# A two-layer decoder trunk on one core: the first layer's head, from the first load to the second chunk of the input projection

## The chip, the cores and the metric

The kernel runs on one core of a Trainium2 chip. Its time is in device microseconds (us), the median of several runs: 663.21 (662.91 to 663.65, three runs). The profile is one further execution, with a time of its own.

## The reference

Two layers over 256 tokens of 1024 channels, float32. Each layer normalises x (RMS norm with a gain), projects it once into 2866 columns, feeds three mixers in parallel from these columns, projects back, adds to x, and runs an MLP with squared ReLU:

```python
for l in range(DEPTH):                       # DEPTH = 2
    h = rms_norm(x, ln1_gain[l])
    proj = h @ w_in[l]                       # (256, 1024) @ (1024, 2866)
    ... = jnp.split(proj, offsets, axis=-1)  # q, six k/v, gates | c_q, c_kv, k_pe | retention q, k, v, gate
    o_nsa = nsa_mixer(partial_rope(nsa_q, cos_p, sin_p), ...)       # compressed, selected, window branches
    o_mla = mla_mixer(mla_cq, mla_ckv, mla_kpe, ..., cos_m, sin_m)  # low-rank queries and keys
    o_ret = retention_mixer(ret_q, ret_k, ret_v, ret_gate, ..., cos_r, sin_r)
    x = x + jnp.concatenate([o_nsa, o_mla, o_ret], axis=-1) @ w_out[l]
    h = rms_norm(x, ln2_gain[l])
    x = x + jnp.square(jax.nn.relu(h @ w_up[l])) @ w_down[l]
return rms_norm(x, final_gain)
```

The rotary tables cos and sin are computed from the positions, for three widths.

## The kernel before, in words

The 256 tokens are two tiles of 128 (t = 0, 1). x stays in SBUF (`xs`, 128 partitions x 2 x 1024). Matmuls in full float32 precision are made of three products (`mm3`, L145): each operand is split into a high part, cast to fp32r on ScalarE (L141), and a low part, the difference, on VectorE (L142); the sum of low x high, high x low and high x high goes into one PSUM bank.

The input projection goes by chunks of columns: A (434: gates, low-rank queries and keys), B2 (384), B1, B3, then the retention's. A chunk's weights come in units (`raw` tiles): A has four, each of two blocks of 128 rows (2 x 434 columns), B2 four of 2 x 384. For each unit and each token tile `inproj` (L549) does two `mm3`, so chunk A is 48 products. Behind A come the low-rank weights uq and uk (scaled by a norm gain and split, L389 and L390), B2, the small loads for the compression (`add_cmp`, L398: sixteen position loads of 8 KB and three of 32 KB), and so on.

`Stream` (L266) holds all units in order. `get` loads up to 12 units ahead of the one asked for, on SyncE's queue, and has those up to four ahead split. Raw tiles have five buffers, split tiles five, and a load waits for a buffer. `hold` and `release` keep splits behind a given instruction. The order of instructions on each engine is made when the program is built, from simulated times and from priorities (`prio`); `tc.issue_after` puts an instruction behind another.

The head, before: SyncE issues the constants `c0s` (with the identity for transposes), half of x's first tile, the gain `g8`, the other half, A's unit 0, x's whole second tile, A's units 1 to 3 (L168 to L180, L324). TensorE does eight warm-up matmuls on a zeroed tile `idle` (L177). `norm_half` (L481) transposes x by 512 channels of a tile: four transposes into a bank, a multiplication by the transposed gain `gT` on VectorE (`xg`, L494), and a split into `xT`. All four halves are done so, in the order (t, h) = (0,0), (0,1), (1,0), (1,1); the sums of squares follow on ScalarE (`sum_sq`, L504), the rows' factors on POOL, and then, in program order ahead of chunk A, the rotary tables (`rope_tables`, L201: some 28 short VectorE instructions and two Sins). Since the normalising factor is applied when a chunk is evacuated (`scaled`, L563), the products need only `xT`. The low parts of A's units 1 and 2 are on POOL (`START_POOL`, L49).

Of the kernel before, what the change touches and what calls it, by code (L numbers as in the profile page):

```python
# [48 lines left out]
START_POOL = (1, 2)  # L49
# [28 lines left out]
def tile_hybrid_trunk(  # L78
# [66 lines left out]
    def mm3(o, a, b, start, stop):  # L145

        nc.tensor.matmul(o, a[1], b[0], start=start, stop=False)  # L147
        nc.tensor.matmul(o, a[0], b[1], start=False, stop=False)  # L148
        nc.tensor.matmul(o, a[0], b[0], start=False, stop=stop)  # L149
# [16 lines left out]

    g8 = scr("g8", [8, P])
    nc.sync.dma_start(c0s, c0)  # L168
    nc.sync.dma_start(xs[:, 0, 0:512], xv[:, 0, 0:512])
    nc.sync.dma_start(g8, ln1_gain[0].rearrange("(k p) -> k p", p=P))  # L170
    nc.sync.dma_start(xs[:, 0, 512:D], xv[:, 0, 512:D])

    idle = scr("idle", [P, P])
    nc.vector.memset(idle, 0.0)
    ps_idle = acc("ps_idle")
    for _ in range(WARM):
        nc.tensor.matmul(ps_idle[:, 0:P], idle, idle, start=True, stop=True)  # L177

    def late_start():
        nc.sync.dma_start(xs[:, 1, :], xv[:, 1, :])  # L180

    nc.gpsimd.dma_start(pos_i, positions.rearrange("o (t p) -> p (o t)", p=P))
# [18 lines left out]
    def rope_tables():  # L201
# [27 lines left out]
        nc.scalar.activation(s1, r, AF.Sin)  # L229
        nc.scalar.activation(s2, r, AF.Sin, scale=0.5)  # L230
        nc.vector.tensor_tensor(u, s2, s2, op=ALU.mult)
        nc.vector.tensor_scalar(u, u, -2.0, 1.0, op0=ALU.mult, op1=ALU.add)
        for off, sl, n in ((0, slice(0, 16, 2), 8), (16, slice(0, 16), 16), (48, slice(16, 48), 32)):
            for half in range(2):
                dst = slice(off + half * n, off + (half + 1) * n)
                nc.vector.tensor_copy(tab_c[:, :, dst], u[:, :, sl])
                nc.vector.tensor_scalar(tab_s[:, :, dst], s1[:, :, sl], 1.0 if half else -1.0, None, op0=ALU.mult)
# [28 lines left out]
    class Stream:  # L266
# [21 lines left out]

        def hold(self, key):

            self.limit = self.index[key]
# [25 lines left out]
    def add_unit(key, pieces, n, eng=nc.vector):  # L317

        name = "_".join(str(z) for z in key)

        def load():
            raw = raw_tile(name)
            for view, src in pieces:
                nc.sync.dma_start(view(raw), src)  # L324
            return raw

        def split_(raw):
            p = hilo(name)
            m = n // PIECES.get('A0' if key[:2] == (0, 'A') else key[1], 1)
            for o in range(0, n, m):  # L330
                split(p[0][:, o:o + m], p[1][:, o:o + m], raw[:, o:o + m], eng)
            return p

        W.add(key, load, split_)
# [12 lines left out]
    def add_chunk(l, name, end=None, first=0):  # L347
        col, n = CHUNKS[name]
        wv = w_in[l].rearrange("(k p) n -> p k n", p=P)
        for i, ks in list(enumerate(KSETS[n]))[first:end]:  # L350
            m = len(ks)
            add_unit((l, name, i), [(lambda r_, m=m, n=n: r_[:, 0:m * n].rearrange("p (k n) -> p k n", k=m),
                                     wv[:, ks[0]:ks[-1] + 1, col:col + n])], m * n,
                     nc.gpsimd if (l, name) == (0, "A") and i in START_POOL else nc.vector)
# [6 lines left out]
    def add_mla(l):  # L361
        def small():
            nrm = p2.tile([P, 4], F32, name=f"l{l}_nrm", tag="nrm")
            nc.sync.dma_start(nrm[:, 0:2], mla_q_norm[l].rearrange("(k p) -> p k", p=P))
            nc.sync.dma_start(nrm[:, 2:3], mla_kv_norm[l].rearrange("(k p) -> p k", p=P))
            return nrm

        add_side(l, "nrm", small)

        def load_uq():  # L370
            raw = raw_tile(f"uq{l}")
            nc.sync.dma_start(raw[:, 0:960].rearrange("p (k n) -> p k n", k=2),
                              mla_w_uq[l].rearrange("(k p) n -> p k n", p=P))
            return raw

        def load_uk():
            raw = raw_tile(f"uk{l}")
# [20 lines left out]
    def add_cmp(l):  # L398
        def small():
            w2s = p1.tile([P, 3, 64], F32, name=f"l{l}_w2s", tag="w2s")  # L400
            pos_t = p1.tile([P, 2, 2, 64], F32, name=f"l{l}_pos_t", tag="pos_t")
            for z, (pe, w2) in enumerate(((cmp_pos_k, cmp_w2_k), (cmp_pos_v, cmp_w2_v))):
                nc.sync.dma_start(w2s[:, 2 * z], w2[l])
                for rep in range(8):
                    nc.sync.dma_start(pos_t[rep * 16:(rep + 1) * 16, z], pe[l].rearrange("(b a) d -> a b d", b=2))
            nc.sync.dma_start(w2s[:, 1], cmp_w2_k[l])
# [40 lines left out]
    for l in range(DEPTH):  # L447
        if l == 0:
            add_chunk(l, "A", 1)
            W.add("x1", late_start)  # L450
            add_chunk(l, "A", 4, 1)
        else:
            add_chunk(l, "A")
        add_mla(l)
        add_chunk(l, "B2")
# [25 lines left out]
    def norm_half(t, h, gain, eng=nc.vector):  # L481
# [3 lines left out]
        if gain is None:  # L485
            for j in range(4):
                nc.tensor.transpose(ps[:, j * P:(j + 1) * P], xs[:, t, h * 512 + j * P:h * 512 + (j + 1) * P], ident)
            if t == h == 0:

                ps_g = acc("ps_g")  # L490
                nc.tensor.transpose(ps_g[:, 0:8], g8, ident[0:8, 0:8])
                nc.vector.tensor_copy(gT, ps_g[:, 0:8])
            xg = xg.rearrange("p (k c) -> p k c", k=4)
            nc.vector.tensor_tensor(xg, ps.rearrange("p (k c) -> p k c", k=4),  # L494
                                    gT[:, 4 * h:4 * h + 4].unsqueeze(2).broadcast_to([P, 4, P]), op=ALU.mult)
            dst = (slice(None), slice(4 * h, 4 * h + 4), slice(t * P, (t + 1) * P))
            return split(xT[0][dst], xT[1][dst], xg)
# [5 lines left out]

    def sum_sq(t, h, ss):  # L504
        junk = scr("junk", [P, 512])
        nc.scalar.activation(junk, xs[:, t, h * 512:(h + 1) * 512], AF.Square, scale=1.0 / 32.0,
                             accum_out=ss[:, t, h:h + 1])
# [9 lines left out]
    for u in W.units[:W.index["x1"] + 1]:  # L517
        u[2] = u[0]()
        W.loaded += 1


    for l in range(DEPTH):
# [7 lines left out]
        if l == 0:  # L530
            for t in range(2):
                for h in range(2):
                    last = norm_half(t, h, None)
            with tc.issue_after(last[0].ins):
                for t in range(2):
                    for h in range(2):
                        sum_sq(t, h, ss1)
        else:
            ss1 = ss_next
        for t in range(2):  # L540
            mean_sq(ms1, ss1, t)
            rsqrt(rstd[:, t:t + 1], ms1[:, t:t + 1])
            nc.gpsimd.tensor_scalar(hrstd[:, t:t + 1], rstd[:, t:t + 1], 0.5, None, op0=ALU.mult)

        if l == 0:
            rope_tables()
        mixT = [p1.tile([P, 8, S], F32R, name=f"{L}mixT{i}", tag=f"mixT{i}") for i in range(2)]

        def inproj(name, evac):  # L549
            n = CHUNKS[name][1]  # L550
            ps = [acc(f"{L}{name}{t}") for t in range(2)]
            for i, ks in enumerate(KSETS[n]):
                w = W.get((l, name, i))
                for t in range(2):
                    tk = slice(t * P, (t + 1) * P)
                    for j, kt in enumerate(ks):
                        mm3(ps[t][:, 0:n], (xT[0][:, kt, tk], xT[1][:, kt, tk]),
                            [z[:, j * n:(j + 1) * n] for z in w], start=kt == 0, stop=kt == 7)
            with prio(name):
                for t in range(2):  # L560
                    evac(t, ps[t][:, 0:n])

        def scaled(o, i, t):  # L563
            nc.scalar.activation(o, i, AF.Copy, scale=rstd[:, t:t + 1])
# [5 lines left out]
        def evac_a(t, ps):  # L570
            a_sb[t] = scr(f"{L}a{t}", [P, W_A], chain="M")
            scaled(a_sb[t], ps, t)

        inproj("A", evac_a)
# [621 lines left out]
```

## Time and profile before

| | |
|---|---|
| median of 3 runs | 663.21 us |
| the profiled execution, its own time | 663.0 us |
| its span | 661.2 us |
| TensorE busy (3619 products) | 640.3 us, 97% |
| VectorE busy | 457.3 us, 69% |
| ScalarE busy | 381.2 us, 58% |
| POOL busy | 73.6 us, 11% |
| chain that ended last | TensorE 89% of the span |

PE is the TensorE matmul, PEld its weight load, DVE VectorE, ACT ScalarE, POOL GpSimd, SPq the queue of SyncE, which issues the loads. A line of a timeline has the start, the time from there to the end of what is merged in it, engine, line of the kernel, operation, out<-in, shape and number; in brackets how long the engine sat idle before it and what ended that. PEclk is the granted clock of TensorE as a share of 2.4 GHz.

### The profile page before, as it was taken

What the parts mean: (1) busy time and instruction counts of PE and PEld (TensorE: products, weight loads), DVE (VectorE), ACT (ScalarE), POOL (GpSimd) and SP (SyncE); (2) the same over time, 40 slices, a digit from 0 to 9 for tenths busy, and PEclk for the clock granted to TensorE, in tenths of its full rate; (3) what the DMA queues carried; (4) which work ended last, traced back from release to release, by engine and by line L of the source; (5) the groups of instructions that cost most, each with busy time, mean ns of one, the idle gap of its engine ahead of it and who ended that gap; (6) DMA issues with size and microseconds to landing.
All of it is one profiled execution on the core that took longest, in us unless ns stands there. A gap on an engine that the chain in (4) does not pass through costs nothing.

```text
span 661.2 us, 10422 instructions
## 1 busy us (share of the span) xinstructions
PE 640.3 (97%) x3619; PEld 550.1 (83%) x3619; DVE 457.3 (69%) x1059; ACT 381.2 (58%) x895; POOL 73.6 (11%) x128
## 2 busy tenths in 40 slices
PE   5999999999999999999999999999999999999995
PEld 4998998677888888888889999968688888888884
DVE  6667988757856666666685698886686666666663
ACT  5868786546644444444466887846474544444442
POOL 3420500310000000000033132130100000000000
PEclk7999999999999999999999999999999999999998
DMA  7877627033756565656547574522275565656521
GB/s 236 253 172 238 199 97 201 33 128 103 252 187 216 166 214 169 204 177 201 147 120 199 179 219 135 142 94 87 74 270 186 183 220 160 218 164 214 169 64 63
DMA packets 79796, 111.64 MB, mean 169 GB/s; under 512 B 9720, under 2 KB 67968, under 8 KB 79616
## 3 DMA queue, kind: packets, MB, share of 16 engines
q1 hardware_dynamic: 79136, 108.89, 53.2%
q0 software_dynamic: 608, 2.10, 0.9%
q8 instruction: 28, 0.46, 0.3%
q14 instruction: 24, 0.20, 0.1%
HBM read 109.92 MB, written 1.05 MB: 168 GB/s over the span
## 4 chain that ended last, share of the span: by engine, by line
PE 89%; DVE 3%; DMA 3%; SPq 2%; POOL 1%; issue 1%; ACT 1%; POOLq 0%; ACTq 0%; DVEq 0%
PE ps_up L1037 18%; PE ps_up L1038 9%; PE l_pd L149 9%; PE l_pd L147 9%; PE l_pd L148 9%; PE l_B L148 2%; PE l_po L147 2%; PE l_B L149 2%; PE l_B L147 2%; PE l_po L149 2%; PE l_po L148 2%; PE l_oT L865 2%; PE ps_pT L873 1%; PE ps_sm L651 1%; DMA raw_uq<-in_mla_w_uq_dram 1%; PE ps_s L812 1%
## 5 line engine op out<-in xcount | busy, mean ns | idle before, releaser
L1037 PE MATMUL ps_up<-xT,hi_wu 128*128 128x512 f32 x512 | 180.9, 397 | 0.4 <-DVE u_s L1049 0.4
L1038 PE MATMUL ps_up<-xT,lo_wu 128*128 128x256 f32 x512 | 141.1, 281 | 0.0
L142 DVE TENSOR_TENSOR lo_wd<-raw_wd,hi_wd 128x1024 fp32r<-128x1024 f32 x64 | 78.2, 1225 | 55.8 <-ACT hi_wd L141 55.6
L1037 PEld LDWEIGHTS ps_up<-xT,hi_wu 128*128 128x128 f32 x512 | 95.8, 188 | 23.6 <-DVE u_s L1049 1.1
L149 PE MATMUL l_pd<-hi_wd,u_h 128*128 128x512 f32 x256 | 100.7, 393 | 0.0
L148 PE MATMUL l_pd<-lo_wd,u_h 128*128 128x512 f32 x256 | 100.0, 391 | 0.0
L147 PE MATMUL l_pd<-hi_wd,u_l 128*128 128x512 f32 x256 | 99.8, 391 | 0.0
L1038 PEld LDWEIGHTS ps_up<-xT,lo_wu 128*128 128x128 f32 x512 | 96.4, 189 | 2.1
L141 ACT CAST hi_wu<-raw_wu 128x512 fp32r<-128x512 f32 x128 | 72.8, 620 | 35.2 <-issue 28.2
L142 DVE TENSOR_TENSOR lo_wu<-raw_wu,hi_wu 128x512 fp32r<-128x512 f32 x128 | 82.1, 685 | 14.7 <-ACT hi_wu L141 14.6
L141 ACT CAST hi_wd<-raw_wd 128x1024 fp32r<-128x1024 f32 x64 | 67.1, 1052 | 36.3 <-PE l_pd L149 22.0
L149 PEld LDWEIGHTS l_pd<-hi_wd,u_h 128*128 128x128 f32 x256 | 48.1, 188 | 10.5
L147 PEld LDWEIGHTS l_pd<-hi_wd,u_l 128*128 128x128 f32 x256 | 48.1, 188 | 10.4
L148 PEld LDWEIGHTS l_pd<-lo_wd,u_h 128*128 128x128 f32 x256 | 48.1, 188 | 9.7
L141 ACT CAST u_h<-u_u 128x512 fp32r<-128x512 f32 x32 | 19.9, 622 | 53.0 <-DVE u_u L1051 52.8
L1048 ACT COPY u_s<-ps_up 128x256 f32<-128x256 f32 x64 | 23.4, 370 | 38.5 <-PE ps_up L1038 38.5
L1049 DVE TENSOR_TENSOR u_s<-ps_up,u_s 128x256 f32<-128x256 f32 x64 | 26.6, 420 | 24.8 <-ACT u_s L1048 24.8
L142 DVE TENSOR_TENSOR lo_B<-raw_B,hi_B 128x192 fp32r<-128x192 f32 (+1 forms) x80 | 29.0, 417 | 20.8 <-ACT hi_B L141 18.9
L829 ACT ACTIVATE p_nsa<-p_nsa,nsa_m 128x256 f32<-128x256 f32 (+2 forms) x72 | 28.6, 400 | 11.0 <-DVE nsa_m L827 10.9
L142 DVE TENSOR_TENSOR u_l<-u_u,u_h 128x512 fp32r<-128x512 f32 x32 | 22.1, 690 | 17.9 <-ACT u_h L141 17.9
L148 PE MATMUL l_B<-lo_B,xT 128*128 128x384 f32 x96 | 32.9, 343 | 0.1
L147 PE MATMUL l_B<-hi_B,xT 128*128 128x384 f32 x96 | 32.8, 349 | 0.0
(320 smaller groups left out, 1233.2 us busy)
## 6 DMA issues: line engine op xcount, KB each, us to landing
raw_wu<-in_w_up_dram SPq DMA_DIRECT2D x64, 512.0 KB, 4.6
raw_wd<-in_w_down_dram SPq DMA_DIRECT2D x64, 512.0 KB, 4.2
raw_B<-in_w_in_dram SPq DMA_DIRECT2D x24, 384.0 KB, 3.6
raw_wo<-in_w_out_dram SPq DMA_DIRECT2D x10, 512.0 KB, 3.5
raw_A<-in_w_in_dram SPq DMA_DIRECT2D x8, 434.0 KB, 4.8
raw_wo<-in_w_out_dram SPq DMA_DIRECT2D x12, 256.0 KB, 4.2
raw_w<-in_cmp_w_k_dram SPq DMA_DIRECT2D x8, 256.0 KB, 4.5
raw_w<-in_cmp_w_v_dram SPq DMA_DIRECT2D x8, 256.0 KB, 4.1
```

What stands on the lines that cost most here:

```text
L141: a = nc.scalar.copy(out=hi, in_=src)
L142: b = eng.tensor_tensor(lo, src, hi.bitcast(F32), op=ALU.subtract)
L147: nc.tensor.matmul(o, a[1], b[0], start=start, stop=False)
L148: nc.tensor.matmul(o, a[0], b[1], start=False, stop=False)
L149: nc.tensor.matmul(o, a[0], b[0], start=False, stop=stop)
L651: nc.tensor.matmul(ps[:, i * 256:i * 256 + nk], qkT[:, 5 + h, t * P:(t + 1) * P], qkT[:, h, 0:nk], start=True, stop=True)
L829: nc.scalar.activation(p[:, o:o + n], p[:, o:o + n], AF.Exp, scale=-1.0, bias=ms[:, r, b:b + 1], accum_out=ls[:, r, b:b + 1])
L865: nc.tensor.matmul(oT[gp, 0:384], kv_sb[kt][:, vi, gp], pTs[g][:, 0:384], start=i == 0, stop=False)
L1037: nc.tensor.matmul(ps[j], w[0][:, o:o + P], x2, start=i == 0 and k == 0, stop=False)
L1038: nc.tensor.matmul(ps[j][:, 0:S], w[1][:, o:o + P], x2[:, 0:S], start=False, stop=i == 1 and k == 3)
L1048: nc.scalar.copy(sj, ps[j][:, S:512])
L1049: nc.vector.tensor_tensor(sj, ps[j][:, 0:S], sj, op=ALU.add)
```

## The change

x comes by halves of the channels. Its first halves (both tiles) are loaded first, then A's units 0 and 1, the second halves, A's units 2 and 3. Three `Line` objects chain the instructions of VectorE, ScalarE and TensorE in a written order up to the first unit of B2; A's weights are split by 434 columns within it, all low parts on VectorE. The transposes of the second halves stand behind the products of A's unit 0. Nine more warm-up matmuls follow the first transposes. A Sin on ScalarE is issued at the start, on a column of the warm-up tile. The rotary tables come behind this order, with Sins that write the tables themselves.

```diff
-    nc.sync.dma_start(c0s, c0)
-    nc.sync.dma_start(xs[:, 0, 0:512], xv[:, 0, 0:512])
-    nc.sync.dma_start(g8, ln1_gain[0].rearrange("(k p) -> k p", p=P))
-    nc.sync.dma_start(xs[:, 0, 512:D], xv[:, 0, 512:D])
+    x_part(0, 0)                  # nc.sync: xs[:, t, h * 512:(h + 1) * 512]
+    nc.scalar.dma_start(c0s, c0)
+    nc.gpsimd.dma_start(pos_i, positions.rearrange("o (t p) -> p (o t)", p=P))
+    x_part(1, 0)
+    nc.scalar.dma_start(g8, ln1_gain[0].rearrange("(k p) -> k p", p=P))
     idle = scr("idle", [P, P])
     nc.vector.memset(idle, 0.0)
+    nc.scalar.activation(idle[:, 0:1], idle[:, 1:2], AF.Sin)
     ps_idle = acc("ps_idle")
-    for _ in range(WARM):
-        nc.tensor.matmul(ps_idle[:, 0:P], idle, idle, start=True, stop=True)
-    def late_start():
-        nc.sync.dma_start(xs[:, 1, :], xv[:, 1, :])
+    warm(WARM)                    # the same 8 matmuls
...
     def rope_tables():
-        nc.scalar.activation(s1, r, AF.Sin)
         nc.scalar.activation(s2, r, AF.Sin, scale=0.5)
         nc.vector.tensor_tensor(u, s2, s2, op=ALU.mult)
-        nc.vector.tensor_scalar(u, u, -2.0, 1.0, op0=ALU.mult, op1=ALU.add)
         for off, sl, n in ((0, slice(0, 16, 2), 8), (16, slice(0, 16), 16), (48, slice(16, 48), 32)):
             for half in range(2):
-                nc.vector.tensor_copy(tab_c[:, :, dst], u[:, :, sl])
-                nc.vector.tensor_scalar(tab_s[:, :, dst], s1[:, :, sl], 1.0 if half else -1.0, None, op0=ALU.mult)
+                nc.scalar.activation(tab_s[:, :, off + half * n:off + (half + 1) * n], r[:, :, sl], AF.Sin,
+                                     scale=1.0 if half else -1.0)
+            for t in range(2):
+                nc.vector.tensor_scalar(tab_c[:, t, off:off + 2 * n].rearrange("p (h n) -> p h n", h=2),
+                                        u[:, t, sl].unsqueeze(1).broadcast_to([P, 2, n]), -2.0, 1.0, ...)
...
+    class Line:
+        def __call__(self, f):
+            with tc.issue_after(self.last.ins) if self.last else nullcontext():
+                self.last = f()
+    vec, act_, ten = Line(), Line(), Line()
+    def start_transposes(t, h):   # four transposes of xs[:, t], each through ten
+    def start_gain(t, h, ps):     # xg = ps * gT, through vec
+    def start_parts(hi, lo, src):
+        act_(lambda: nc.scalar.copy(out=hi, in_=src))
+        vec(lambda: nc.vector.tensor_tensor(lo, src, hi.bitcast(F32), op=ALU.subtract))
+    def start_x(t, h, xg):        # start_parts of xg into xT
+    def start_w(i, j):            # start_parts of half j (434 or 384 columns) of unit i
...
         if l == 0:
-            for t in range(2):
-                for h in range(2):
-                    last = norm_half(t, h, None)
-            with tc.issue_after(last[0].ins): ...     # the four sum_sq
+            W.hold((0, "B2", 0))
+            ps = [start_transposes(0, 0)]
+            ps_g = acc("ps_g")
+            ten(lambda: nc.tensor.transpose(ps_g[:, 0:8], g8, ident[0:8, 0:8]))
+            vec(lambda: nc.vector.tensor_copy(gT, ps_g[:, 0:8]))
+            act_(lambda: sum_sq(0, 0, ss1))
+            ps.append(start_transposes(1, 0))
+            ten(lambda: warm(WARM_ON))                # WARM_ON = 9
+            xg = [start_gain(t, 0, ps[t]) for t in range(2)]
+            start_x(0, 0, xg[0]); start_w(0, 0); start_w(0, 1)
+            start_x(1, 0, xg[1]); start_w(1, 0); start_w(1, 1)
+            act_(lambda: sum_sq(1, 0, ss1))
-        if l == 0:
-            rope_tables()
+        def start_rest(ss1=ss1):                      # called behind unit 0's products
+            ps = [start_transposes(t, 1) for t in range(2)]
+            xg = [start_gain(t, 1, ps[t]) for t in range(2)]
+            for t in range(2): start_x(t, 1, xg[t])
+            for i in (2, 3):
+                for j in range(2): start_w(i, j)
+            for t in range(2): act_(lambda: sum_sq(t, 1, ss1))
+            factors()                                 # mean_sq, rsqrt, hrstd
+            W.load_to(LOAD_AHEAD)                     # the first 12 units
+            for j in range(2): start_w(4, j)          # B2's unit 0
+            W.release((act_.last, vec.last), SPLIT_AHEAD)
+            W.hold((0, "B2", 2))
...
-        inproj("A", evac_a)
+        last = inproj("A", evac_a)    # unit 0's products go through ten; PSUM banks of att, not acc
+        if l == 0:
+            W.release((last, vec.last), SPLIT_AHEAD)
+            with tc.issue_after(act_.last.ins), tc.issue_after(vec.last.ins):
+                rope_tables()
```

Beside it: the raw tiles of layer 0's A lie in the space of `mixT` (written much later), those of its uq and uk in that of the probabilities; in both layers one unit of B2 stands ahead of uq and uk in the stream, and the loads of `nrm` (gains of the low-rank norms) and `w2s` (second compression weights) are issued by POOL instead of SyncE.

## Rows read from the trace of the kernel before

**Rows 1.** busy time by stretch (us from:to, length; busy us and number by engine)

```profile
0.00:14.46 14.46, 7.18 (x34) 6.32 (x34) 8.45 (x31) 6.58 (x9) 3.24 (x7) 0.79 0.81 262
14.46:26.16 11.70, 11.70 (x50) 11.02 (x51) 9.57 (x21) 9.43 (x23) 5.10 (x9) 0.82 0.70 181
22.60:51.80 29.20, 29.05 (x178) 27.65 (x176) 16.24 (x47) 21.00 (x57) 8.80 (x22) 1.00 0.78 213
60.00:80.00 20.00, 20.00 (x141) 19.94 (x140) 18.74 (x57) 17.26 (x53) 8.62 (x16) 1.00 0.73 220
337.30:347.10 9.80, 9.80 (x52) 9.34 (x51) 7.46 (x15) 8.89 (x22) 2.66 (x7) 1.00 0.44 121
347.10:372.00 24.90, 24.90 (x159) 24.20 (x157) 14.25 (x43) 17.94 (x54) 8.38 (x20) 1.00 0.64 165
```

**Rows 2.** the start in order of time (start, us; in brackets idle before)

```profile
0.74 1.28 ACT L141 ACT_TABLE_LOAD   x1 [0.74 <-PEq L1182]
1.06 3.78 PE L177 MATMUL ps_idle<-idle 128*128 128x128 f32 x16 [1.06 <-DVE idle L174]
1.19 0.42 SPq L169 DMA_DIRECT2D xs<-in_x_dram  x1
1.26 0.90 POOL L182 DMA_DIRECT2D pos_i<-in_positions_dram  x1 [0.81 <-POOLq L1182]
4.63 0.83 PE L487 MATMUL ps_xT<-c0s,xs 128*128 128x128 f32 x4
7.51 0.92 ACT L141 CAST hi_A<-raw_A 128x868 fp32r<-128x868 f32 x1 [5.48 <-DMA raw_A<-in_w_in_dram]
8.94 1.97 PE L487 MATMUL ps_xT<-c0s,xs 128*128 128x128 f32 x8 [1.88 <-DMA xs<-in_x_dram]
9.89 2.48 DVE L494 TENSOR_TENSOR xg<-ps_xT,gT 128x512 f32<-128x512 f32 x4
10.99 1.28 ACT L229 ACT_TABLE_LOAD   x1
12.65 1.12 ACT L141 CAST xT<-xg 128x512 fp32r<-128x512 f32 x2
13.63 1.28 DVE L142 TENSOR_TENSOR xT<-xg,xT 128x512 fp32r<-128x512 f32 x2
```

**Rows 3.** who waited for whom, 0 to 30 us (total, times, longest)

```profile
PE l_A L147 <- DVE xT L142: 3.5, 1, 3.5
```

**Rows 4.** granted clock in half microseconds (columns of group 1, PEclk behind POOL)

```profile
8.50:9.00 0.50, 0.06 (x1) 0.06 (x1) 0.50 (x2) 0.00 (x0) 0.00 (x0) 0.50 1.04 392
18.50:19.00 0.50, 0.50 (x3) 0.47 (x3) 0.50 (x3) 0.50 (x2) 0.15 (x1) 0.76 0.59 98
```

**Rows 5.** timeline of TensorE, two products that lie three apart

```profile
16.40 0.57 PE L149 MATMUL l_A<-hi_A,xT 128*128 128x434 f32 x1
17.49 0.56 PE L149 MATMUL l_A<-hi_A,xT 128*128 128x434 f32 x1
```

**Rows 6.** durations by line (ns min/median/max), the warm-up and a later transpose

```profile
L177 PE MATMUL ps_idle<-idle x16: 421/421/582, 1.1 to 4.4; 128*128 128x128 f32 x16
L500 PE MATMUL ps_xT<-c0s,xg x16: 270/272/300, 334.8 to 337.1; 128*128 128x128 f32 x16
```

**Rows 7.** busy time on the rotary tables' tile (VectorE, ScalarE)

```profile
5.60:20.00 14.40, 4.86 (x28) 0.46 (x2) 0.64 0.88 273
```

**Rows 8.** groups by line, 0 to 30 us (busy us, mean ns)

```profile
L142 DVE TENSOR_TENSOR lo_A<-raw_A,hi_A 128x868 fp32r<-128x868 f32 x2 | 2.1, 1051 | 0.0
L141 ACT CAST hi_A<-raw_A 128x868 fp32r<-128x868 f32 x4 | 3.6, 912 | 7.1 <-DMA raw_A<-in_w_in_dram 7.1
L506 ACT ACTIVATE junk<-xs 128x512 f32<-128x512 f32 x4 | 2.5, 624 | 0.0
L389 ACT ACTIVATE hi_uq<-raw_uq,l_nrm 128x480 fp32r<-128x480 f32 x2 | 1.3, 682 | 0.0
```

**Rows 9.** loads of A's units, issue to landing

```profile
DMA to landing us min/median/max: 5.0/6.9/7.3
```

More of the change, by code (lines that the diff above doesn't have):

```diff
@@ L287, in get, with load_to @@
             return u[3] if u[1] else u[2]
+        def load_to(self, n):
+            while self.loaded < n:
+                u = self.units[self.loaded]
+                u[2] = u[0]()
+                self.loaded += 1
         def hold(self, key):
@@ L315, in hilo, with add_unit @@
         return [splitp.tile([P, 1024], F32R, name=f"{z}_{name}", tag=z) for z in ("hi", "lo")]
-    def add_unit(key, pieces, n, eng=nc.vector):
+    homes = {}
+    def add_unit(key, pieces, n, home=None, part=0):
         name = "_".join(str(z) for z in key)
         def load():
-            raw = raw_tile(name)
+            if home:
+                if home not in homes:
+                    homes[home] = p1.tile([P, 2, 1024], F32, name="raw_" + home, tag=home)
+                raw = homes[home][:, part]
+            else:
+                raw = raw_tile(name)
             for view, src in pieces:
@@ L328, in split_ @@
             p = hilo(name)
-            m = n // PIECES.get('A0' if key[:2] == (0, 'A') else key[1], 1)
+            m = n // PIECES.get(key[1], 1)
             for o in range(0, n, m):
-                split(p[0][:, o:o + m], p[1][:, o:o + m], raw[:, o:o + m], eng)
+                split(p[0][:, o:o + m], p[1][:, o:o + m], raw[:, o:o + m])
             return p
@@ L353, in add_chunk @@
                                      wv[:, ks[0]:ks[-1] + 1, col:col + n])], m * n,
-                     nc.gpsimd if (l, name) == (0, "A") and i in START_POOL else nc.vector)
+                     home=f"mixT{i // 2}" if (l, name) == (0, "A") else None, part=i % 2)
     def add_side(l, name, f):
@@ L484, in norm_half @@
         ps = wk("ps_xT", "MN"[h])
[L485 to L497, printed above, removed]
         eng.tensor_tensor(xg, xs[:, t, sl], gain[:, sl], op=ALU.mult)
@@ L515, in split_mix @@
         split(mixT[0][dst], mixT[1][dst], src)
-    for u in W.units[:W.index["x1"] + 1]:
+    for i, u in enumerate(W.units[:4]):
+        if i == 2:
+            x_part(0, 1)
+            x_part(1, 1)
         u[2] = u[0]()
@@ L550, in inproj @@
             n = CHUNKS[name][1]
-            ps = [acc(f"{L}{name}{t}") for t in range(2)]
+            if (l, name) == (0, "A"):
+                ps = [att(f"{L}{name}{t}", "MN"[t]) for t in range(2)]
+            else:
+                ps = [acc(f"{L}{name}{t}") for t in range(2)]
             for i, ks in enumerate(KSETS[n]):
-                w = W.get((l, name, i))
+                start = (l, name, i) == (0, "A", 0)
+                w = W.units[0][3] if start else W.get((l, name, i))
                 for t in range(2):
```

112 lines of the change are left out of this document (80 added, 32 removed).

## The prediction

> **What bounds the kernel now.** I read the busy time by stretch first [rows 1]. TensorE is the bound almost everywhere: it is busy 24.90 of 24.90 us in the stretch of layer 1 that follows chunk A there. The exception is the start. Up to 14.46 us, where the first product of chunk A begins, it works 7.18 us, and on warm-up and transposes only. The next 11.70 us hold the 48 products of chunk A at a mean granted clock of 0.82; the same 48 take 9.80 us in layer 1, with weights and x at hand [rows 1]. So against layer 1 the head has 1.9 us of slow clock to give, and what lies ahead of 14.46.
>
> The second view is the start in order of time [rows 2]. The warm-up runs from 1.06, the first transposes at 4.63, the last eight wait for x until 8.94. VectorE multiplies by the gain only from 9.89, since it has rotary tables in hand till then, and does all four pieces first. ScalarE loads a table at 10.99 for the Sin and casts the first x only at 12.65. The last link is the subtraction at 13.63, for which TensorE waits 3.5 us [rows 3].
>
> The third view is the clock [rows 4]. It is recorded as 0.50 from 8.5, after TensorE's pause for x, and as 1.00 from about 18.7, after products without a pause since 14.46. At 0.50 three products take 1.09 us [rows 5], 0.363 each; layer 1's take 0.20 (9.80 over 48). Durations correct the record at the very start, where it also says 1.00 (the mean of 0.79 up to 14.46 is 8.5 us at 1.00 and the rest at 0.50): a warm-up record takes 421 ns, a transpose of the same 128x128 at full clock 273 [rows 6]. So the warm-up runs at 1.2 GHz.
>
> **The change, step by step.** All times are of the profiled execution: span 661.2, its own time 663.0, which is 0.2 under the median of 663.21.
>
> *Warm-up.* The new Sin on ScalarE writes a column of the tile that the warm-up matmuls read, so they now wait for it, and everything on TensorE is queued behind them. Ahead of it ScalarE has two DMA issues and the table load. It issues no DMA in this trace; SyncE's took 0.42, POOL's 0.90 [rows 2]. I take SyncE's, as the transfer is of its kind, and keep as bounds nothing (if the load runs under them) and 0.90. The Sin itself is 0.23 (two took 0.46, [rows 7]). 0.74 + 2 x 0.42 + 1.28 + 0.23 = 3.1, bounds 2.3 and 4.1. Eight matmuls are 16 records in 3.78 us, so they end at 6.9 instead of 4.84: the change loses 2 us here by itself. It buys the load at 10.99, which goes.
>
> *First halves.* x's first halves are issued first, where one such piece was issued at 1.19 and in use at 4.63, so they are there by 6.9. Four transposes (0.83), the gain's and four more follow. VectorE copies the gain at about 7.9 and is then the path, in its fixed order: copy (to 8.1), two gains of 0.68 as in the group of 2.48 for four (9.5), the first x's low part 0.64 (10.1), two low parts of A's unit 0, the second x, two low parts of unit 1. A low part of 434 columns is worked out from 0.64 for 512 and 1.05 for 868 [rows 2, 8]: 0.55. So unit 0 is split at 11.2, the second x at 11.9, unit 1 at 13.0. ScalarE's casts (0.56 and half of 912 ns) stay ahead of it, with 0.8 for a sum of squares (0.62, [rows 8], and its read-out) in its waits. Nine more warm-ups are 18 records: 4.2 us at half clock, 2.1 at full, which I take, since TensorE has then worked from 3.1 without a pause; they end at 10.5, hidden under VectorE until 11.2. If they run at half, see rival 2. Unit 0's last six products need the second x at 11.9 and end at 13.1, at full clock, as no pause of TensorE is left that is like the one before 8.9.
>
> *Transfers.* A's unit 0 landed at 7.51 behind 604 KB; it has the same 604 KB ahead of it now, fewer issues on SyncE, and its use comes at 9.5. Units 2 and 3 landed at most 7.3 us after their issue [rows 9]; they are now the seventh and eighth load, at 0.42 to 0.5 each issued before 5, so there by 12.3, and used at 16. x's second halves have one unit more (434 KB) ahead of them than the x that came at 8.94; at the 392 GB/s of these microseconds [rows 4] that is 1.1 us, so 10.1, for a use at 13.1. All are hidden; without that cover a microsecond late is one lost.
>
> *Second halves.* Their eight transposes stand behind unit 0 on TensorE (0.9, to 14.0), unit 1 follows to 16.4. VectorE: two gains from 13.7 (15.1), two x (16.4), unit 2 (17.5), unit 3 (18.6). Unit 2 stops for low parts at 16.9 and 17.5 and ends at 19.2, unit 3 at 21.6, where chunk A ended at 26.16: 4.5 us gained.
>
> *What is moved behind.* ScalarE's two sums (1.6) and B2's first unit (0.9, by columns) end at 20.2, VectorE's share at 20.8, in front of B2's start at 21.6. The query and key weights uq (1.27, [rows 8]) and uk (0.85, by columns) take ScalarE to 22.3. Before, it had just this list done at 22.6, so ScalarE has gained nothing while TensorE is 4.5 ahead. B2's second unit follows on ScalarE to 23.3 and on VectorE to 24.3, and TensorE wants it at 23.7: 0.6 lost. The rotary tables come on top. VectorE did 28 instructions in 4.86 us for them [rows 7]; twelve short writes become six, so some 4.5. ScalarE has 7 Sins of 0.23, 1.6 us. They lay in the wait for x; now they lie beside B2. I charge 0.5 for that. Its bounds are a gain of 0.7, if the stretch from 26.16 to 51.80 comes down from its 25.64 to its like in layer 1, 24.90 [rows 1], and the loss of all 4.5 (rival 4).
>
> *At nothing:* the small loads that leave SyncE for POOL (0.90 each, and POOL has lost the subtractions of A); raw A in mixT's tiles, uq and uk in those of the probabilities, so B2 is loaded right behind A and no buffer holds it, with the sixteen small position loads behind it; and layer 1's order, where one B2 unit goes ahead of uq under 9.80 us of products. These could cost or give 0.3 in all.
>
> **Sum:** 4.5 - 0.6 - 0.5 = 3.4; 663.0 - 3.4 = 659.6, and by the 0.2 between profile and median I say 659.7. I carry the gain through to the end, as TensorE is busy 20.00 of 20.00 between 60 and 80 us [rows 1] and waits there for nothing that would swallow it.
>
> **Rivals.**
>
> 1. *The Sin doesn't hold TensorE* (12%). For it: the load could run under the DMA issues; against: the matmuls read the column. The warm-up then starts at 1.06 and VectorE's path at 5.9, all up to 2.2 earlier, as A allows it (landed by 7.5, wanted at 7.4): 657.4.
>
> 2. *The clock rises later* (9%), and transposes and nine warm-ups still run at 1.2 GHz. They then end at 13.1, unit 0 at 15.4, and the second halves are 2.2 later: 661.9. For it: only one rise stands in these rows. Against: ahead of that one TensorE had worked without a pause, as it will have here. The Trainium skill (TensorE: Matmul & The Clock Gate, "What's actually happening") says that the point of the rise isn't tied to the kernel's start and so varies; by that rule this rival is what happens now and then, and no row here shows it.
>
> 3. *The second transposes come behind unit 1* (8%), if the order on TensorE is made with x later than it is. VectorE then idles from 13.0 to 16.0, unit 2 starts 2.3 later, A ends at 23.9: 662.0.
>
> 4. *ScalarE becomes the bound from chunk A to the compression product at 51.8* (15%, the slower side). From 22.6 to 51.8 it was busy 21.00 of 29.20 us, 72% [rows 1]. It has the same to do from 22.3, with 1.6 of Sins, and two more table loads (2.56) if the gates' Exp comes between the Sins: 25.2. For the whole gain that must fit into 24.9 us, which it can't; without the loads, 22.6, it fits at 91% busy. It turns into a loss where it is under 85% busy (25.2 of the 29.5 to 51.8). At 80%, between that and the 72 of before, it takes 31.5 us, 2.0 beyond 51.8: 665.2. Against it: its idle time there was mostly waiting for TensorE, and the tables aren't wanted before B2's evacuation.
>
> **How the numbers follow.** My forecast has 56%: 659.7, with 658.3 to 661.2 of its own. 0.2% is 1.3 us, about what a measurement of this kernel tells from no change: faster is under 661.9, slower over 664.5. Faster: 0.56 + 0.12 + half of rivals 2 and 3 (0.09) + 0.01 of rival 4 = 0.78. Slower: 0.12 of rival 4. The rest, 0.10, is the same. The range, 657.0 to 662.9, holds the forecast, most of rival 1 and rivals 2 and 3, and leaves out rival 4 and a tail of rival 1.
>
> **What would show it.** The first warm-up near 3.1 and the first gain on VectorE near 8; near 1 and 6, it is rival 1. Products of unit 0 at 0.20 apart; at 0.363, rival 2. The second transposes between units 0 and 1; else rival 3. B2's first product at 21.6, and the compression product near 48.4; if that is near 51.8 with ScalarE hardly idle before it, rival 4. The main step is wrong if B2 begins less than 3 us earlier; what I say of the rest is wrong if B2 does and the end moves by less than 2.

## The result: slower, and the profile after

The changed kernel takes 667.09 us (median of 5 runs, 666.58 to 669.86), the kernel before beside it 663.44: a ratio of 1.0061, interval 1.0043 to 1.0079, so 0.6% slower and clear of the noise. Forecast were 659.7 us and a range of 657.0 to 662.9. The profiled execution has a span of 664.5 us, against 661.2, and TensorE is busy 643.8 us in it, against 640.3.

The head did what the change says. Its timeline (the answer to [rows 2]; columns as there):

```profile
1.80 1.28 ACT L180 ACT_TABLE_LOAD   x1 [1.80 <-issue]
3.09 0.20 ACT L180 ACTIVATE idle<-idle 128x1 f32<-128x1 f32 x1
3.35 3.78 PE L185 MATMUL ps_idle<-idle 128*128 128x128 f32 x16 [3.35 <-ACT idle L180]
6.92 1.06 PE L527 MATMUL ps_xT<-c0s,xs 128*128 128x128 f32 x4
8.42 1.32 DVE L532 TENSOR_TENSOR xg<-ps_xT,gT 128x512 f32<-128x512 f32 x2
8.85 2.17 PE L185 MATMUL ps_idle<-idle 128*128 128x128 f32 x18
10.78 0.44 PE L147 MATMUL l_A<-hi_start,xT 128*128 128x434 f32 x1
13.58 1.04 PE L527 MATMUL ps_xT<-c0s,xs 128*128 128x128 f32 x8
21.89 0.51 PE L147 MATMUL l_B<-hi_start,xT 128*128 128x384 f32 x2
35.70 0.49 PE L147 MATMUL l_B<-hi_B,xT 128*128 128x384 f32 x1 [3.35 <-ACT l_kc L660]
53.42 1.98 PE L832 MATMUL ps_h<-raw_w,l_T 128*32 128x128 f32 x64
```

Chunk A's first product comes at 10.78 instead of 14.46 and B2's at 21.89 instead of 26.19, 4.3 us earlier. But the compression product comes at 53.42; the stretch in [rows 1] that ends with it ended at 51.80. So between B2's start and that product the change loses 5.9 us. The same time by stretches, cut at the pause (from:to, length; busy and number of PE, PEld, DVE, ACT, POOL; granted clock, DMA share, GB/s; columns as in [rows 1] and [rows 4]):

```profile
10.78:21.89 11.11, 11.05 (x59) 9.89 (x58) 9.52 (x22) 8.91 (x21) 2.27 (x4) 1.00 0.86 279
21.89:32.35 10.46, 10.46 (x61) 9.87 (x60) 6.36 (x23) 6.95 (x22) 2.26 (x4) 1.00 0.60 177
32.35:35.70 3.35, 0.01 (x1) 0.01 (x1) 2.60 (x11) 2.75 (x10) 0.00 (x0) 1.00 1.09 377
35.70:39.45 3.75, 3.75 (x13) 3.75 (x14) 2.42 (x14) 3.63 (x13) 0.46 (x3) 0.54 1.24 233
39.45:53.42 13.97, 13.53 (x86) 12.15 (x85) 6.45 (x21) 9.59 (x23) 6.32 (x18) 1.00 0.61 133
```

Third row: TensorE stands still for 3.35 us. Fourth row: behind that pause the granted clock falls to 0.50, its level of 1.2 GHz (the row's mean is 0.54), and twelve products come 0.32 us apart instead of 0.175, 1.7 us more. Together 5.05 of the 5.9. Of the rest, 0.44 us is waiting in the fifth row (13.97 less 13.53 busy), and three transposes (`ps_cT`) stand behind B2's first product that stood ahead of it before.

Why it stands still is read backwards, from the timelines of ScalarE and then of SyncE (SPq):

```profile
28.53 0.33 ACT L686 ACTIVATE l_gate<-l_gate 128x18 f32<-128x18 f32 x2
32.34 1.11 ACT L141 CAST hi_B<-raw_B 128x192 fp32r<-128x192 f32 x4 [3.48 <-DMA raw_B<-in_w_in_dram]
34.05 1.11 ACT L141 CAST hi_B<-raw_B 128x192 fp32r<-128x192 f32 x4 [0.60 <-DVE lo_B L142]
35.07 0.57 ACT L660 ACTIVATE l_kc<-l_B,l_rstd 128x384 f32<-128x384 f32 x1
36.66 1.28 ACT L236 ACT_TABLE_LOAD   x1
```

```profile
11.61 4.17 SPq L345 DMA_DIRECT2D raw_B<-in_w_in_dram  x3
15.82 5.19 SPq L429 DMA_DIRECT2D l_pos_t<-in_cmp_pos_k_dram  x8
21.06 3.68 SPq L429 DMA_DIRECT2D l_pos_t<-in_cmp_pos_v_dram  x8
24.78 0.42 SPq L478 DMA_DIRECT2D c1s<-c_dram  x1
25.25 0.43 SPq L345 DMA_DIRECT2D raw_B<-in_w_in_dram  x1
```

TensorE waits for `l_kc`, B2's evacuation, which frees the PSUM bank for B1. ScalarE takes its instructions in order, and in front of `l_kc` stand the casts of B1's units 0 and 1; unit 0 lands only at 32.3. It was issued at 25.25, as SyncE issues sixteen position loads of 8 KB ahead of it in one block, from 15.82 to 24.74. While it does, the DMA engines have little to do, a share of 0.20 after against 0.75 before. After and then before, 20 to 26 us, columns as above:

```profile
20.00:26.00 6.00, 6.00 (x38) 5.86 (x36) 6.00 (x20) 6.00 (x16) 1.57 (x4) 1.00 0.20 32
```

```profile
20.00:26.00 6.00, 6.00 (x32) 5.69 (x32) 4.13 (x9) 3.73 (x8) 2.33 (x6) 1.00 0.75 197
```

In the kernel before, the position loads stood among B2's loads, which are L324 here (nine of SyncE's rows, the last the unit's own, and one of ScalarE's). The unit was issued at 25.16 and cast at 32.74, which was in time, as TensorE was late itself:

```profile
12.29 2.43 SPq L405 DMA_DIRECT2D l_pos_t<-in_cmp_pos_k_dram  x5
14.82 0.39 SPq L324 DMA_DIRECT2D raw_B<-in_w_in_dram  x1
15.26 0.93 SPq L405 DMA_DIRECT2D l_pos_t<-in_cmp_pos_k_dram  x2
17.23 0.38 SPq L324 DMA_DIRECT2D raw_B<-in_w_in_dram  x1
17.66 1.40 SPq L405 DMA_DIRECT2D l_pos_t<-in_cmp_pos_v_dram  x3
19.63 0.38 SPq L324 DMA_DIRECT2D raw_B<-in_w_in_dram  x1
20.95 0.38 SPq L324 DMA_DIRECT2D raw_B<-in_w_in_dram  x1
21.38 1.40 SPq L405 DMA_DIRECT2D l_pos_t<-in_cmp_pos_v_dram  x3
25.16 0.38 SPq L324 DMA_DIRECT2D raw_B<-in_w_in_dram  x1
32.74 1.12 ACT L141 CAST hi_B<-raw_B 128x192 fp32r<-128x192 f32 x4 [0.36 <-DMA raw_B<-in_w_in_dram]
```

### The profile page after: what moved, and what is told of

The parts are those of the page before. It is cut to its first block, busy times and chain, and to the rows that moved or that the text cites. A ratio compares the mean times of both kernels' runs of the same rounds, so it can differ in the third digit from the quotient of the medians.

```text
span 664.5 us, 10471 instructions
## 1 busy us (share of the span) xinstructions
PE 643.8 (97%) x3637; PEld 551.3 (83%) x3637; DVE 455.2 (69%) x1058; ACT 383.0 (58%) x906; POOL 73.9 (11%) x136
## 2 busy tenths in 40 slices
DMA packets 78564, 111.64 MB, mean 168 GB/s; under 512 B 8264, under 2 KB 66512, under 8 KB 78384
## 5 line engine op out<-in xcount | busy, mean ns | idle before, releaser
L142 DVE TENSOR_TENSOR lo_B<-raw_B,hi_B 128x192 fp32r<-128x192 f32 (+1 forms) x78 | 27.3, 400 | 22.0 <-ACT hi_B L141 21.8
L929 ACT ACTIVATE p_nsa<-p_nsa,nsa_m 128x256 f32<-128x256 f32 (+2 forms) x72 | 28.6, 399 | 11.1 <-DVE nsa_m L927 11.0
```

Source lines behind the costliest of these rows:

```text
L142: b = eng.tensor_tensor(lo, src, hi.bitcast(F32), op=ALU.subtract)
L929: nc.scalar.activation(p[:, o:o + n], p[:, o:o + n], AF.Exp, scale=-1.0, bias=ms[:, r, b:b + 1], accum_out=ls[:, r, b:b + 1])
```

## Experiments

Ratios are to the kernel before, with their intervals; the changed kernel has 1.0061. Every edit is made on it.

**The queue, the PSUM banks, ScalarE, the head: one edit each.**

```diff
-                    nc.sync.dma_start(pos_t[rep * 16:(rep + 1) * 16, z], ...)
+                    (nc.gpsimd if l == 0 else nc.sync).dma_start(pos_t[rep * 16:(rep + 1) * 16, z], ...)
```

> Edit: layer 0's sixteen position loads are issued by POOL instead of SyncE. Theory S (SyncE issues them in one block of about 9 us ahead of B1's unit 0, so that unit is issued at 25.25 and lands at 32.3, eight microseconds after TensorE would have it; ScalarE's order then holds B2's evacuation behind B1's casts): unit 0 of B1 is issued before 20 and lands before 26, the wait of 3.35 us before 35.70 goes, and with it the 12 products at half clock (0.32 instead of 0.175 us, 1.7 us): 667.1 - 5.0 = 662.1, between 661 and 663.5. Theory R (ScalarE has too much to do from chunk A to B2's end, with seven Sins and two more table loads): the loads change nothing of that, the wait for B2's evacuation on ScalarE stays, 666.5 to 667.5. Theory Q (the wait is for the PSUM banks of B2 alone): as R.

664.19 us, 1.0001 [0.9987, 1.0015]. SyncE issues B1's unit 0 at 16.42 instead of 25.25. The pause before B1 is gone, with the slow clock, and the compression product comes at 51.4 instead of 53.4. So the queue is a cause. But 662 wasn't reached. B2 starts at 21.9 and now another pause shows, on ScalarE:

```profile
22.66 0.62 ACT L660 ACTIVATE l_a<-l_A,l_rstd 128x434 f32<-128x434 f32 x1
26.58 0.28 ACT L236 ACTIVATE rt<-rt 128x96 f32<-128x96 f32 x1 [3.30 <-DVE rt L235]
26.77 0.20 ACT L240 ACTIVATE tab_s<-rt 128x16 f32<-128x16 f32 x1
26.88 0.60 ACT L660 ACTIVATE l_a<-l_A,l_rstd 128x434 f32<-128x434 f32 x1
27.54 0.55 PE L693 MATMUL ps_cT<-c0s,l_a 128*128 128x128 f32 x3 [0.98 <-ACT l_a L660]
```

The first Sin of the rotary tables waits 3.30 us for VectorE's angles, and chunk A's second evacuation is queued behind it; TensorE then waits 1.0 us for `l_a` and 1.4 for what hangs on it.

```diff
-            if (l, name) == (0, "A"):
+            if (l, name) in ((0, "A"), (0, "B1")):      # PSUM banks of att
```

> Edit: layer 0's B1 accumulates in the PSUM banks of the attention, so its products needn't wait for the evacuation of B2; nothing else changes. Theory Q: the wait of 3.35 us before 35.70 goes, and the half clock behind it: 662. Theory S: the data are late as well. Unit 0 of B1 lands at 32.3, its high part is cast by 33.4 and its low part is there at 33.6; TensorE stops at 32.35 for 1.0 to 1.3 us instead of 3.35, and the clock may still fall: 664.5 to 666. Theory R: ScalarE is the bound, so the time comes back at B1's next unit: 666.5 to 667.5.

```profile
32.43 0.44 PE L147 MATMUL l_B<-hi_B,xT 128*128 128x384 f32 x1 [1.60 <-ACT hi_B L141]
```

TensorE resumes at 32.43 instead of 35.70, after 1.60 us of waiting for a cast of B1's unit: the bank made the pause longer, the late unit made it. Past that the run says nothing of the change: the order of the whole program comes out otherwise, and it takes 683.72 us (1.0295 [1.0273, 1.0318]), most of it lost behind the compression product, which comes at 53.4 again.

```diff
-        nc.scalar.activation(s2, r, AF.Sin, scale=0.5)
-        nc.vector.tensor_tensor(u, s2, s2, op=ALU.mult)
+        nc.gpsimd.memset(tab_s, 0.5)
+        nc.vector.tensor_tensor(u, r, r, op=ALU.mult)
...                                                     # and the six Sins into tab_s left out
```

> Edit: the rotary tables are filled without their seven Sins (tab_s is a constant, tab_c a polynomial of the reduced angle), so ScalarE loses the Sins and the two table loads that they bring between the gates' Exp (left out: the sine of the positions). Theory R: ScalarE has about 1.6 + 2.6 us less to do between chunk A and the compression product, the wait before 35.70 goes or nearly so: 662 to 664. Theory S: unit 0 of B1 still lands at 32.3, the wait stays within 0.5 us of its 3.35; at most the 0.5 us of Sins ahead of B2's evacuation goes: 666.3 to 667.1.

666.00 us, 1.0034 [1.0020, 1.0049]; the wait is 2.9 us:

```profile
35.34 0.45 PE L147 MATMUL l_B<-hi_B,xT 128*128 128x384 f32 x1 [2.92 <-ACT l_kc L657]
```

That is as the queue's theory had it, with 0.3 us more gained: the Sins and their table loads aren't what TensorE waits for.

```diff
-    nc.scalar.activation(idle[:, 0:1], idle[:, 1:2], AF.Sin)
+    first = const.tile([P, 2], F32, name="first")
+    nc.vector.memset(first, 0.0)
+    nc.scalar.activation(first[:, 0:1], first[:, 1:2], AF.Sin)
```

> Edit: the Sin at the start writes a tile of its own, so the warm-up needn't wait for it (the first rival of the prediction). Theory S: the head ends about 2 us earlier (B2's first product near 19.9 instead of 21.89), but SyncE's block of position loads still sets when unit 0 of B1 lands (within 0.5 us of 32.3), so TensorE only waits longer before its first product of B1, and the time stays within 0.5 us of 667.1. Rival (what is saved ahead is kept, and the loss behind it is a fixed one): 665.

666.94 us, 1.0044 [1.0029, 1.0059]. A starts at 8.3, B2 at 19.7, and TensorE's pause grows to what was saved and more:

```profile
36.74 0.69 PE L147 MATMUL l_B<-hi_B,xT 128*128 128x384 f32 x1 [6.56 <-ACT l_kc L662]
```

This is the plainest of the four: a head 2.2 us shorter gives nothing while the loads set when B1 can begin.

**Tables ahead of the head, alone and with the loads moved; layer 1's order.**

```diff
+            rope_tables()                               # was behind the written order
             ps = [start_transposes(0, 0)]
```

> Edit: the rotary tables are computed ahead of the head's written order (VectorE is idle from 1.0 to 8.2 there), not behind it; the loads stay as they are. If the place of the tables is the cause by itself: the two table loads behind chunk A become one and no Sin stands between evacuations, so TensorE's wait before B1's first product goes: 662 to 663.5. If the queue of SyncE is the cause by itself: unit 0 of B1 still lands at 32.3, the wait stays between 2.5 and 3.5 us, and the time is that of the run without Sins, 666.0, give or take 0.5; up to 1 us more where the tables' last writes on VectorE push the first gain back.

> Edit: both: the position loads on POOL and the rotary tables ahead of the head's order. If two causes stand one behind the other (the late unit, then the Sins that hold chunk A's second evacuation for 3.3 us): both waits go, TensorE works without a pause from chunk A to the compression product, which comes near 48 instead of 51.4: 660 to 661.5. If they only add up (2.9 and 1.1 us): 663. If something else is short there, by ScalarE's amount of work: 664, as with the position loads on POOL alone.

> Edit: the tables ahead of the head's order; the position loads stay on SyncE, but behind B1's units in the stream instead of ahead of them. If only the place of the block counts: unit 0 of B1 is issued before 18 and lands before 25, units 1 to 3 come behind the block at about 26 at the earliest, as they wait for buffers anyway: within 1 us of the run with the loads on POOL. If the number of issues on SyncE counts wherever they stand: the wait moves to unit 1, 663 to 666.

664.34 (1.0019 [1.0010, 1.0028]), 665.33 (1.0024 [1.0015, 1.0034]) and 664.66 us (1.0020 [1.0011, 1.0028]). The positions land at 6.3 to 6.4 and in the first the tables then hold VectorE until 11.1, so A starts at 13.1 to 13.3 and B2 at 24.4 to 25.9. From there to the compression product the three take 26.1, 26.5 and 26.2 us, with no wait of over 0.4 (the change: 31.5). The first does so with the block of loads in place, as TensorE is late again. The stretch can be run without a pause, then, but these runs give the head back for it. The first lies between its two theories, the second misses all of its (660 to 664). The third is where it was expected if only the place of the block counts, within 1 us of the 664.19 of the first experiment, but also within the 663 to 666 of the other theory, so its time doesn't decide; B1's unit 0 is issued ahead of the block there and no wait moved to unit 1, as the first theory has it.

```diff
-        add_chunk(l, "B2", 1)
+        if l == 0:
+            add_chunk(l, "B2", 1)
         add_mla(l)
-        add_chunk(l, "B2", 4, 1)
+        add_chunk(l, "B2", 4, 0 if l else 1)            # and layer 1's nrm, w2s on SyncE again
```

> Edit: layer 1's order of loads as before the change (uq and uk ahead of all of B2, the small loads of layer 1 on SyncE); layer 0 as after. From layer 1's chunk A to the end it takes 317.5 us after and 316.4 before. If the new order of loads makes the difference: 1 us less, 666.0. If the difference comes from how the order of instructions falls out there (it is 316.8 to 317.6 in the runs so far, with that order of loads in all): within 0.5 us of 667.1, with no less in layer 1.

665.99 us, 1.0037 [1.0024, 1.0049], with 317.7 us from layer 1's chunk A to the end. Layer 1 is no shorter, so the order of loads there isn't what costs its 1 us; the 1.1 us by the medians lie in no stretch that I could name.

**Four ways that failed.** Tables on POOL with the Sins in ScalarE's gap; position loads behind B1's unit 3 on SyncE; both; both with the Sin's own tile.

```diff
+        eng = nc.gpsimd                                 # rope_angles(): the angles on POOL
...
             act_(lambda: sum_sq(1, 0, ss1))
+            rope_sins(*angles, act_)
```

> Edit: the angles and the cosine tables are computed on POOL (idle from 6.4 to 19.2), two small steps excepted, and the seven Sins stand on ScalarE in its gap at 12.7 to 14.9; the loads stay as after. The run with the tables ahead of the head paid about 2.4 us on VectorE for them (first product of A at 13.3 instead of 10.8). Theory of two causes (late unit of B1, and the Sins between the evacuations): A starts at 10.8 and B2 at 21.9 as after, the wait for unit 0 of B1 (3 us) and part of the slow clock stay: 665 to 666. If the Sins alone are the cause: 661.

```diff
+                    with nullcontext() if l else tc.issue_after(loads[0, "B1", 3].ins):
                       nc.sync.dma_start(pos_t[rep * 16:(rep + 1) * 16, z], ...)
```

> Edit: the position loads stand behind the load of B1's unit 3 on SyncE; the tables stay as after. Theory of two causes: unit 0 of B1 lands before 25, but the Sins hold chunk A's second evacuation as they did with the loads on POOL (3.3 us there, of which TensorE lost 1.0 and 1.4): 663.5 to 664.5. If the queue alone is the cause: 661.

> Edit: both of the two before: tables on POOL, position loads behind B1's unit 3. Theory of two causes: B2 starts at 21.9, TensorE works from there to the compression product without a wait of over 0.5 us, in the 26.1 to 26.5 us that it took in the three runs with the tables first: 48.2, against 51.8 before. Layer 1 as in the other runs, 0.4 to 2 us longer than before: 660 to 662. If ScalarE's and VectorE's amount of work is the bound from chunk A on (the prediction's rival 4), the stretch grows to 28 or more and the time is 663 to 664.5.

> Edit: as the run with both, and the Sin at the start writes a tile of its own, so the warm-up doesn't wait for it; the seven Sins stand behind the splits of A's unit 3. Theory of two causes: the head gives its 2.2 us (A's first product at 8.3), and what the late unit swallowed of it before is now kept: 658 to 660. If the loads or ScalarE are short again this much earlier: 660 to 662, with a wait between B2 and the compression product.

663.72 (1.0020 [1.0009, 1.0030]), 665.03 (1.0034 [1.0022, 1.0045]), 667.64 (1.0074 [1.0062, 1.0086]) and 666.88 us (1.0065 [1.0053, 1.0078]): none has the number of a theory, the second misses by 0.5. Each put a new wait into an in-order queue. With the tables on POOL, the Sin waits for POOL's angles until 16.84, with the casts of x's second half behind it, TensorE pauses 2.3 us in chunk A, and the clock is at 0.50 from 20 to 23 us. With the position loads later on SyncE (they also come behind B1 in the stream), they stand ahead of the first compression weights (`raw_w`) and of B3's unit 0 instead, which lands at 49.98 in the last of the four. ScalarE's rows of the first and of the last:

```profile
16.84 0.28 ACT L243 ACTIVATE rt<-rt 128x96 f32<-128x96 f32 x1 [4.10 <-POOL rt L237]
```

```profile
49.98 1.11 ACT L141 CAST hi_B<-raw_B 128x192 fp32r<-128x192 f32 x4 [6.14 <-DMA raw_B<-in_w_in_dram]
```

**Both causes out at little cost in the head.** Position loads as two of 16 partitions and three copies that double them, on POOL; angles on VectorE, nine steps ahead of the gain's copy and six in its gap behind A's unit 1; Sins behind the sums of squares, cosine tables on POOL. Then also layer 1's position loads behind the retention's last unit; then also the Sin's own tile.

```diff
+                nc.gpsimd.dma_start(pos_t[0:16, z], ...)
+            for n in (16, 32, 64):
+                nc.gpsimd.dma_start(pos_t[n:2 * n], pos_t[0:n])
```

> Edit: layer 0's position loads are two loads of 16 partitions and three copies that double them, on POOL; the angles are computed on VectorE in its idle time, nine steps before the gain's copy at 8.2 and six in the gap at 13.1; the Sins stand behind the sums of squares on ScalarE, the cosine tables on POOL behind the rows' factors. So neither SyncE's queue nor an in-order wait for the Sins is left, and the head doesn't pay for the tables. Theory of two causes: A at 10.8 to 11.2, B2 at 21.9 to 22.3, then 26.1 to 26.5 us to the compression product: 48.5, 3.3 earlier than before the change; 660 to 661 with 0.4 to 1 lost in layer 1. Theory of a third bound (the transfers themselves: in the trace of the run with both loads and tables moved, the DMA share is over 1 from 38 to 48 us, and B3's first unit lands only then): a wait appears at 40 to 54 us, and the time is 662 to 664.

> Edit: as the run before, and layer 1's sixteen position loads, which the order on SyncE puts between B3's and the retention's units of layer 0 (44 to 58 us), stand behind the retention's last unit. If these issues hold up B3's units: 0.5 to 2 us less than the run before. If not: the same within 0.5 us, as the loads there wait for buffers anyway.

> Edit: as the run before, and the Sin at the start has a tile of its own, all angles in VectorE's gap behind A's unit 1. Theory of two causes: A at 8.3, B2 at 19.7 to 20.5, 1.5 to 2.2 us less than the run before, 658 to 659.5. Third bound: the compression product comes no earlier than in the run before, as its weights and B3's first unit wait for buffers and for the transfers ahead of them; the same within 0.7 us.

662.05 (0.9977 [0.9965, 0.9989]), 660.99 (0.9961 [0.9949, 0.9974]) and 661.98 us (0.9984 [0.9974, 0.9994]). Here the kernel is faster than before for the first time. B2 to the compression product takes 26.3, 26.1 and 26.3 us, and no third bound shows; A still starts at 12.3 and 12.2 in the first two, as the positions land at 7.7 and 7.5, and the third pauses 2.4 us within A. So the first misses its 660 to 661 and the third both of its theories; the second is 1.1 us under the first, as expected if layer 1's issues hold up B3's units.

**The positions as the first load.** They then land at 3.2, all angle steps fit ahead of the gain's copy, the Sins ahead of the first cast. First with both causes out, then with the Sin's own tile as well, then the tables alone, with the block of position loads left on SyncE.

```diff
+    nc.sync.dma_start(pos_i, ...)
     x_part(0, 0)
-    nc.gpsimd.dma_start(pos_i, ...)
```

> Edit: as the run with layer 1's loads behind (position loads doubled on POOL), but the positions are the first load of SyncE, all fifteen angle steps stand on VectorE ahead of the gain's copy, the seven Sins on ScalarE ahead of the first cast of x, and the cosine tables on POOL. Theory of two causes: if the positions are there by 5.3, A starts at 10.8 to 11.2 (12.2 in the run before it), B2 at 21.9 to 22.4, the compression product comes at 48.0 to 48.6, and the time is 659.2 to 660.2, 1 to 1.7 less. Third bound (transfers or buffers hold the compression product at 49 to 50): within 0.5 of that run's 661.0.

> Edit: as the run before with the first Sin on a tile of its own. VectorE then has the angles in front of the gain's copy, so A can start at about 9.5 rather than 8.3: 1 us less than the run before if nothing behind is short (658.2 to 659.2), the same within 0.5 if the transfers are.

> Edit: the tables as in the two runs before, but all position loads as after (one block on SyncE). Theory of two causes: the head and B2's start as after (10.8, 21.9), unit 0 of B1 lands at 32.3 as after, TensorE waits 2.5 to 3.3 us for it; about what the run without Sins gave, 665.5 to 666.5. If the tables were the main cause: under 664.

660.48 (0.9960 [0.9947, 0.9972]), 659.07 (0.9945 [0.9933, 0.9957]) and 662.97 us (1.0001 [0.9988, 1.0013]). The first has the head of the changed kernel and no wait of over 0.25 us behind it; its waits from 3 to 54 us, and its stretch from B2 to the compression product:

```profile
PE ps_idle L185 <- ACT idle L180: 3.4, 1, 3.4
PE l_B L147 <- ACT hi_B L141: 0.2, 1, 0.2
```

```profile
21.88:47.85 25.97, 25.72 (x157) 24.33 (x156) 16.99 (x48) 20.71 (x60) 11.61 (x24) 1.00 0.64 177
```

25.97 us instead of 31.5. Its time misses the 659.2 to 660.2 by 0.3 although the compression product comes even earlier than expected (47.85): layer 1 takes 318.05 us there, 1.65 more than before the change. The second is the fastest: the edit that gave nothing on the changed kernel gives 1.4 us here, as the loads no longer decide. The third missed its 665.5 to 666.5. Its SyncE and TensorE:

```profile
24.23 0.43 SPq L354 DMA_DIRECT2D raw_B<-in_w_in_dram  x1
34.80 0.44 PE L147 MATMUL l_B<-hi_B,xT 128*128 128x384 f32 x1 [1.91 <-ACT l_kc L674]
```

Its pause is 1.9 us (B1's unit 0 lands at 29.7, unit 1 at 33.2), not 2.5 or more. Two things shorten it: unit 0 is issued a microsecond earlier than in the changed kernel (24.23, 25.25), and with the tables ready three products of `ps_uk` stand in front of the pause. From B2's start to the compression product it takes 29.8 us, where the changed kernel takes 31.5. As the edit moves the unit's issue as well, the run doesn't show what the tables cost by themselves.

The compression product comes at 53.4 in the changed kernel, at 51.4 with the loads alone moved, at 51.7 with the tables alone moved and at 47.9 with both (the first run here): each edit alone gives about 2 us there, both give 5.6. By ratio, either edit alone brings the kernel back to the time of before (1.0001 twice), and both together, with layer 1's loads behind as well, below it (0.9960).

## Why the prediction was wrong

**What held.** The Sin holds TensorE until 3.35 (forecast 3.1), the first gain is at 8.42 (8), the second transposes stand between units 0 and 1, A's products come 0.20 apart, and B2 begins at 21.89 (21.6). Of 4.5 us, 4.3 came. Rivals 1 to 3 are out. The charge of 0.6 for B2's second unit was not needed: TensorE doesn't pause from B2's start until 32.35.

**The step that failed** is "At nothing": "B2 is loaded right behind A and no buffer holds it, with the sixteen small position loads behind it", for 0.3 in all. It counted the transfers' bytes and buffers, not the issues of the queue and what is queued behind them. In the kernel before, the sixteen issues lay between 8.9 and 22.8 us, among B2's loads, the last of which was issued at 20.95. In the changed kernel B2's last load is issued by 15.8, and the issues became one block of 8.9 us behind it, ahead of B1. That B1's unit 0 would then be issued no earlier than before (25.25, 25.16) while TensorE wants it 4.3 us earlier could have been estimated from the queue's timeline: five issues took 2.43 us there and three 1.40, so sixteen take some 7.7. The price was the pause and the clock behind it, 5.05 us, more than the gain of 4.3.

The Trainium skill (Trainium Kernel Development and Optimization, "Key Constraints") says that issuing DMAs from several engines only saves the sequencer's issue time. The trace agrees, and here this time was the matter: with the sixteen issues on another engine, the DMA engines moved no more bytes (111.65 MB, 111.64 in the changed kernel) and the pause went.

**A term that was too small** is the 0.5 for the rotary tables. Without the Sins the changed kernel takes 1.1 us less (666.00, 667.09), and with the position loads out of the way TensorE loses 2.4 us to the tables' order (0.98 and 1.41 in the first experiment). Rival 4 came nearest in its time (665.2), but not by its mechanism. Its two more table loads came (at 27.24 and 36.66), yet ScalarE wasn't short of time: it is idle for 3.48 us ahead of 32.34. What the tables cost is order: a Sin that waits for VectorE's angles, with an evacuation queued behind it (3.30 us in the first experiment), and tables so late that POOL waits for them until 38.99. In the changed kernel that lateness is itself in part the late unit's: VectorE's angle steps stand behind the unit's low parts there, for which it sits idle 4.48 us before 32.72.

**What stays open.** Of the 3.2 us that the last product comes later (656.9 and 653.7), 1.6 are there at the compression product, 2.1 at layer 1's chunk A; layer 1 adds 1.1. So half of the loss isn't explained by the pause, and the prediction's carrying the gain through to the end, with layer 1's order "at nothing", failed as well: by its own sign, B2 came over 3 us earlier and the end didn't follow. Layer 1 takes 316.4 us before, 317.5 after and 316.8 to 318.5 in the experiments (the one with B1 in the attention's banks left out), 317.7 in the fastest. Most of what differs from run to run lies between its compression product and the retention's first product (13.5 us before, 14.1 after, 15.1 at most); of the 14.14 us after, TensorE waits only 0.08, so it isn't a pause there. Which part of the new order makes them wasn't found.

A rival for the late unit was left untested: SyncE issues `c1s` (1056.5 KB) at 24.78, right ahead of B1's unit 0, which then takes 7.1 us to land. No run puts that load behind the unit, so how much of its lateness is the transfer ahead of it isn't shown.

## What to carry to other kernels

When a stage is made earlier, list what its successor needs and read when each of these is issued, not only when it would be moved: a load that was in time only because TensorE was late has lost its cover. Count a queue's instructions with their issue time, and look at what waits disappear from it, since what was spread among waits becomes a block. An instruction that can wait, such as a Sin for tables nobody needs yet, doesn't belong into an in-order queue ahead of an evacuation.

## What was not expected of the hardware

The 256 positions, 4 bytes each, landed at 5.7 to 7.7 us when POOL issued them at 1.26, and at 3.24 to 3.31 as SyncE's first load. The angle steps that VectorE does 0.25 us apart come some 0.55 us apart on POOL. And a pause of 1.9 us of TensorE (the tables alone) was followed by the lower clock, 0.50 from 36 to 39 us, as was one of 2.3 us (the tables on POOL). Pauses of 1.0 and 1.4 us (the position loads on POOL) were not, and neither was one of 2.4 us within chunk A (the third of the runs with doubled loads), where the granted clock stays at 1.00. So in these runs the length of a pause alone doesn't tell whether the clock falls behind it.
